# A depthwise convolution split by channels between TensorE and VectorE

## The chip, the cores and the metric

The kernel runs on one core of a Trainium2 chip. The metric is the device time of one execution in microseconds; several runs of a kernel are given by their median. A core has five engines that run side by side, each strictly in the order of its own instruction list, and that wait for each other by semaphores: TensorE (PE; PEld is its loading of weights), VectorE (DVE), ScalarE (ACT), GpSimd (POOL) and SyncE (SP), which here issues transfers.

## The reference

A network of two blocks on 512 tokens of width 1024. The first block (window attention beside a state space model, then a feed-forward with retrieved experts) isn't touched. The second has two layers, each a feed-forward, a mixer with four branches over one projection of the normed input, and a feed-forward. The branches are sparse attention with an index and a top-k ("dsa"), gated linear attention ("gla"), a convolution, and latent attention ("mla"). The branch that is changed, of 256 channels and 31 taps:

```python
def conv_mixer(u, w_dw, b_dw, g_norm):
    a, gate = jnp.split(u, 2, axis=-1)
    h = a * jax.nn.sigmoid(gate)
    h = lax.conv_general_dilated(h, w_dw, window_strides=(1,), padding=[(C_KERNEL - 1, 0)],
                                 feature_group_count=C_CHANNELS, ...) + b_dw
    return jax.nn.silu(rmsnorm(h, g_norm))

def hybrid_layer(x, ...):
    x = x + 0.5 * swiglu(rmsnorm(x, ffn1_norm), ...)
    z = rmsnorm(x, mix_norm) @ w_in                       # split into the branches' inputs
    ...
    y = jnp.concatenate([y_a, y_b, y_c, y_d], axis=-1) @ w_out
    x = x + y
    return x + 0.5 * swiglu(rmsnorm(x, ffn2_norm), ...)
```

Each channel has its own 31 taps: output channel c at token t is a sum over k of tap k of channel c times the same channel's input at token t - 30 + k.

## The kernel before

**Layout.** Activations lie with channels on the 128 partitions and the 512 tokens along the row, so a tile is 128x512 float32 and 256 channels are two tiles ("chunks"). A projection to 128 outputs goes over 8 chunks of the input; each operand is split in a high and a low part of a type that PE takes in one pass, and `mm3` makes three products per chunk, 128x128 by 128x512: high by high (L195), high by low (L196), low by high (L197). A weight block comes by `lw` (L999): a transfer by SP into `wr`, a cast on ACT to `wh` (L1009), a subtraction to `wl` on DVE or POOL (L1010). `wr`, `wh` and `wl` have two buffers each. Products that aren't split are plain float32.

**The mixer** (L1050) runs the steps of a list, `ORDER` (L816): hp, ik, t3, iq, exp, index, lat, mla_in, conv, bqk, v3, gla_in and so on to the four dsa steps, then the output projection "wo". `hp` is `conv_in` (L1519): projection blocks 13 and 15, then 14 and 16, and the gating into `hp`, one tile for both chunks with 30 zero columns ahead of the tokens. `ik`, `t3`, `iq` and `lat` project ("win") and keep a block by a DVE multiplication (`keep`, L1066). `index` makes 24 products (L1234), each followed by a ReLU on ACT (L1236) and a weighting on DVE (L1239, L1241); every fourth is preceded by four copies of queries on ACT (L1232). `topk` (L1251, L1252) is a loop of max and replace on DVE, 16 rounds for each of three blocks. `mla_in` makes the latents' products ("mlain"), `conv` (L1532) is the convolution, both chunks on DVE. `conv_norm` sums squares with a product of ones ("convn"), `silu` works on the gates and the convolution (L1120), and L1303 loads a table of ACT's functions.

**What sets the order.** The steps are written in `ORDER`, but what is printed into each engine's list is chosen by a scheduler with its own estimates of durations, over the whole mixer: an engine's instructions of different steps are interleaved, so `conv` on DVE lies between operations of the index and the projections. A few instructions on ACT, the table loads among them, are held in program order. On the chip nothing is reordered any more. PSUM banks are handed out by tags: "pa" for the projections, "pb", "pc" and "pd" for the branches.

## Time and profile before

| | us |
|---|---|
| Runs, median (lowest to highest of 3) | 3793.75 (3792.79 to 3800.03) |
| The profiled execution | 3798.33 |
| its span, first to last instruction | 3796.5 |
| the first mixer, from its first projection to the last output product | 319.6 |
| the second mixer | 318.2 |
| mean granted clock of TensorE | 0.978 |

The two mixers take 638 of 3796 us. Busy times of an engine are the union of its records; a product's record lasts until its result is out, so records of PE that follow each other closely overlap, and the pace of a row is read from the starts. PEclk is the clock that PE was granted, as a share of 2.4 GHz.

### The profile page before, as it was taken

How to read it: one execution, taken by the hardware profiler on the slowest of the kernel's cores; microseconds unless marked ns; L12 is line 12 of the kernel's file. 1: busy time of each engine (PE TensorE's matmuls, PEld its weight loads, DVE VectorE, ACT ScalarE, POOL GpSimd, SP SyncE). 2: the span in 40 equal slices, each digit the busy share in tenths (PEclk: the TensorE clock that was granted, in tenths of full speed). 3: DMA queues.
4: the chain of work that ended last, by engine and by line, in shares of the span. 5: the costliest groups of instructions: out<-in, count | busy, mean ns of one | idle time of the engine just before them, and what ended most of it. 6: DMA issues, size and time to landing. Idle time of an engine off the chain costs nothing.

```text
span 3796.5 us, 46092 instructions
## 1 busy us (share of the span) xinstructions
PE 3622.3 (95%) x17229; PEld 2972.5 (78%) x17229; DVE 2579.3 (68%) x4508; ACT 1410.8 (37%) x2401; POOL 1087.4 (29%) x677
## 2 busy tenths in 40 slices
PE   7798979899999999999999899999999998999999
PEld 6656879778988888878887576888788875767887
DVE  8668989788888889844445987444444459874443
ACT  3253359423333333342223446222322234463222
POOL 4424767445555555530002212000100013210000
PEclk8899989999999999999999999999999999999999
DMA  4212225888888788723222111223232231112233
GB/s 118 77 39 99 75 98 219 300 290 306 299 295 300 284 309 297 275 93 94 93 96 92 51 45 56 95 95 94 92 95 91 95 94 59 45 51 90 94 95 100
DMA packets 182080, 529.88 MB, mean 140 GB/s; under 512 B 22112, under 2 KB 73888, under 8 KB 163680
## 3 DMA queue, kind: packets, MB, share of 16 engines
q1 hardware_dynamic: 157840, 389.36, 30.9%
q0 software_dynamic: 18944, 134.75, 9.6%
q10 hardware_dynamic: 5072, 2.81, 0.3%
q8 instruction: 136, 2.23, 0.2%
q14 instruction: 88, 0.72, 0.1%
HBM read 495.51 MB, written 30.18 MB: 138 GB/s over the span
## 4 chain that ended last, share of the span: by engine, by line
PE 70%; DVE 10%; issue 2%; DMA 2%; ACT 1%; POOL 1%; ACTq 0%; POOLq 0%; SPq 0%; DVEq 0%
PE ps L197 13%; PE ps L196 13%; PE ps L195 13%; PE V L1820 11%; PE S L195 3%; PE S L197 3%; PE S L196 3%; DVE cv L1541 2%; PE G L1755 2%; PE win L197 1%; PE win L195 1%; PE win L196 1%; DVE ds L1241 1%; DMA gt<-gates 1%; PE wo L195 1%
## 5 line engine op out<-in xcount | busy, mean ns | idle before, releaser
L1009 ACT ACTIVATE wh<-wr 128x1024 fp32r<-128x1024 f32 (+1 forms) x334 | 347.3, 1040 | 1058.3 <-PE ps L196 743.2
L197 PE MATMUL ps<-x,wl 128*128 128x512 f32 x1408 | 557.7, 396 | 0.0
L195 PE MATMUL ps<-x,wh 128*128 128x512 f32 x1408 | 557.4, 396 | 0.0
L196 PE MATMUL ps<-x,wh 128*128 128x512 f32 x1408 | 557.3, 396 | 0.0
L989 POOL TENSOR_TENSOR s<-s,s 128x512 f32<-128x512 f32 x42 | 67.4, 1605 | 1163.9 <-ACT s L987 1152.6
L1811 POOL TENSOR_TENSOR vl<-vr,vh 128x1024 fp32r<-128x1024 f32 x128 | 324.5, 2536 | 182.8 <-ACT vh L1810 181.5
L1010 DVE TENSOR_TENSOR wl<-wr,wh 128x1024 fp32r<-128x1024 f32 (+1 forms) x288 | 343.9, 1194 | 44.4 <-ACT wh L1009 37.7
L197 PE MATMUL S<-pxh,ul 128*128 128x384 f32 x1024 | 350.1, 342 | 9.5 <-POOL ul L1772 9.5
L195 PE MATMUL S<-pxh,uh 128*128 128x384 f32 x1024 | 349.3, 341 | 0.1
L196 PE MATMUL S<-pxl,uh 128*128 128x384 f32 x1024 | 348.9, 341 | 0.0
L195 PEld LDWEIGHTS ps<-x,wh 128*128 128x128 f32 x1408 | 265.5, 189 | 64.6 <-ACT ml L947 1.1
L196 PEld LDWEIGHTS ps<-x,wh 128*128 128x128 f32 x1408 | 265.6, 189 | 63.7 <-issue 0.5
L197 PEld LDWEIGHTS ps<-x,wl 128*128 128x128 f32 x1408 | 265.4, 189 | 63.8 <-issue 0.7
L1820 PE MATMUL V<-vl,ah 128*128 128x512 f32 x768 | 302.8, 394 | 10.3 <-POOL vl L1811 10.2
L1820 PE MATMUL V<-vh,ah 128*128 128x512 f32 x768 | 300.8, 393 | 10.8 <-ACT vh L1810 10.8
L1820 PE MATMUL V<-vh,al 128*128 128x512 f32 x768 | 302.8, 394 | 1.3 <-DVE al L181 1.3
L197 PE MATMUL ps<-ml,wl 128*128 128x512 f32 x704 | 278.0, 395 | 0.0
L195 PE MATMUL ps<-ml,wh 128*128 128x512 f32 x704 | 278.0, 395 | 0.0
L1035 DVE TENSOR_TENSOR s<-ps,rs 128x512 f32<-128x512 f32 x88 | 60.9, 692 | 305.1 <-PE ps L197 305.1
L1881 POOL DMA_INDIRECT rows<-in_uv_dram,gidx x128 | 189.6, 1481 | 259.8 <-DVE acc L1890 229.8
L1047 DVE SCALAR_TENSOR_TENSOR hT<-ps,hT 128x512 f32<-128x512 f32 x96 | 66.4, 692 | 269.1 <-PE ps L197 269.1
L1772 DVE TENSOR_TENSOR ul<-ur,uh 128x1024 fp32r<-128x1024 f32 x100 | 187.9, 1879 | 61.6 <-ACT uh L1770 61.5
(578 smaller groups left out, 7919.3 us busy)
## 6 DMA issues: line engine op xcount, KB each, us to landing
wr<-in_f_gu_dram SPq DMA_DIRECT2D x176, 512.0 KB, 3.7
ur<-in_ut_dram SPq DMA_DIRECT2D x128, 512.0 KB, 5.5
vr<-in_uv_dram SPq DMA_DIRECT2D x128, 512.0 KB, 4.8
wr<-in_f_dn_dram SPq DMA_DIRECT2D x64, 448.0 KB, 3.3
gates<-gst SPq DMA_DIRECT2D x12, 2048.0 KB, 6.9
gt<-gates SPq DMA_DIRECT2D x32, 768.0 KB, 6.9
wr<-in_w_dram SPq DMA_DIRECT2D x46, 512.0 KB, 3.4
wr<-in_f_dn_dram SPq DMA_DIRECT2D x32, 512.0 KB, 3.6
```

What stands on the lines that cost most here:

```text
L195: mm(out, wh, xh, start=start, stop=False)
L196: mm(out, wh, xl, start=False, stop=False)
L197: mm(out, wl, xh, start=False, stop=stop)
L989: nc.gpsimd.tensor_tensor(sq, acc, sq, op=OP.add)
L1009: nc.scalar.activation(hi, raw, AF.Copy)
L1010: (eng or nc.vector).tensor_tensor(lo, raw, hi.bitcast(F32), op=OP.subtract)
L1541: V.scalar_tensor_tensor(a, hp[:, m, k:k + T], dw[:, m, k:k + 1], a, op0=OP.mult, op1=OP.add)
L1755: nc.tensor.matmul(pt[:, t], b[:, t], a, start=True, stop=True)
L1772: e.tensor_tensor(ul, raw, uh.bitcast(F32), op=OP.subtract)
L1811: nc.gpsimd.tensor_tensor(vl, raw, vh.bitcast(F32), op=OP.subtract)
L1820: nc.tensor.matmul(ps[k], x[:, ts], y[:, cs], start=b == 0 and n == 0, stop=b == P - 1 and n == 2)
L1881: nc.gpsimd.indirect_dma_start(r, None, self.A["uv"], bass.IndirectOffsetOnAxis(ap=self.gi[:, s:s + 1], axis=0))
```

## The change

In both mixers the first 128 channels of the convolution (chunk 0) go from DVE to PE, and the other 128 (chunk 1) stay as they were.

- `conv` becomes `conv1` and `conv0`. `conv1` is the old loop for chunk 1. `conv0` makes for each tap k a 128x128 matrix with the tap's 128 weights on the diagonal (ACT scales the identity by a column) and multiplies it with the input shifted by k, in float32; 31 products add up in one PSUM bank ("pd"), and ACT copies the sum out with the bias. The matrices lie in a ring of four within one tile of the tag "sd". `conv0` is called after `conv1`.
- `conv_in` makes chunk 1 first. The two weight blocks that are loaded ahead of the mixer are 14 and 16; 13 and 15 have their low parts on DVE, and 14 and 16 on POOL. `hp` is two tiles, and the taps' transfer is issued at its start.
- `ya`, which reuses the memory of `hp`, is two tiles as well.

All else in the scheduled order follows from this. ACT's list now holds three more table loads between the convolution's norm and the output projection, since the norm's logarithm (L202) and exponential (L203) come to stand between the SiLUs (L1126).

```diff
@@ -1050,12 +1050,12 @@
     def mixer(self, l, x):
         net, nc, w, p = self.net, self.nc, self.w, self.p
         V = nc.vector
-        first = {b: self.lw(self.A["w2"][l, b], 1024) for b in (13, 15)}
+        first = {b: self.lw(self.A["w2"][l, b], 1024) for b in (14, 16)}
         xh, xl, rx = self.scaled(x, "mix")
 
         def proj(b):
             wh, wl = (a.rearrange("p (c m) -> p c m", c=NCH)
-                      for a in first.pop(b, None) or self.lw(self.A["w2"][l, b], 1024, nc.vector if b in (14, 16) else nc.gpsimd))
+                      for a in first.pop(b, None) or self.lw(self.A["w2"][l, b], 1024, nc.vector if b in (13, 15) else nc.gpsimd))
             ps = net.ps("pa", "win")
             for c in range(NCH):
                 net.mm3(ps, (wh[:, c], wl[:, c]), (xh[c], xl[c]), c == 0, c == NCH - 1)
@@ -1103,13 +1103,19 @@
 
         def mla(j):
             if "ya" not in v:
-                v["ya"] = p.tile([P, 2, T + 30], F32, tag="hp", name=net.nm("ya"))[:, :, :T]
+                v["ya"] = [p.tile([P, T + 30], F32, tag=f"hp{m}", name=net.nm("ya"))[:, :T] for m in (1, 0)]
             with net.banks("pb", "mla"):
                 self.mla(j, v["mla"], v["ya"])
 
         def qkn():
             with net.banks("pc", "qkn", rsc):
                 v["rq"] = self.qk_norm(v["qk"])
+        def conv():
+            h0, h1, dw = v["hp"]
+            a = self.conv1(h1, dw)
+            with net.banks("pd", "conv"):
+                v["acc"] = [self.conv0(h0, dw), a]
 
         def conv_norm():
             with net.banks("pd", "convn", rsc):
@@ -1130,7 +1136,7 @@
                     src = v["gla"][m]
                     V.tensor_mul(src, src, v["rg"][m])
                 else:
-                    src = v["ya"][:, m]
+                    src = v["ya"][m]
                 net.split(src, yh[k], yl[k])
 
         def dsa(j):
@@ -1141,7 +1147,7 @@
                 self.dsa(j, v["masks"][j], v["qk"], v["rq"], vt, yh, yl, ("sm", "sd")[j % 2])
 
         steps = {
-            "hp": lambda: v.update(hp=self.conv_in(proj, rx)),
+            "hp": lambda: v.update(hp=self.conv_in(l, proj, rx)),
             "exp": self.exp_set,
             "t3": lambda: v.update(t3=keep(3, "t3")),
             "iq": lambda: v.update(iq=[keep(0, "ds"), keep(1, "ds")]),
@@ -1151,7 +1157,7 @@
             "mla_in": mla_in,
             "bqk": lambda: v.update(bqk=[keep(8, "gl"), keep(9, "gl")]),
             "gla_in": gla_in,
-            "conv": lambda: v.update(acc=self.conv(l, v["hp"])),
+            "conv": conv,
             "qk": lambda: v.update(qk=[keep(b, "ds") for b in (4, 5, 6, 7)]),
             "qkn": qkn,
             "gla": gla,
@@ -1404,7 +1410,7 @@
                 nc.scalar.activation(sm[h][:, :j * P], ps[:, :j * P], AF.Identity, scale=r)
             V.scalar_tensor_tensor(sm[h][:, ts], ps[:, ts], r, self.caus, op0=OP.mult, op1=OP.add)
         self.softmax_pv(sm, n, lambda k, h: kv[k][:, 256 + h * 64:256 + (h + 1) * 64],
-                        lambda c, po: nc.scalar.activation(ya[:, c, ts], po, AF.Copy))
+                        lambda c, po: nc.scalar.activation(ya[c][:, ts], po, AF.Copy))
 
     def gla_in(self, l, bq, bk, t3):
         net, nc, w, p = self.net, self.nc, self.w, self.p
@@ -1516,30 +1522,43 @@
             out.append(o)
         return out
 
-    def conv_in(self, proj, rx):
+    def conv_in(self, l, proj, rx):
         net, nc, w, p = self.net, self.nc, self.w, self.p
-        hp = p.tile([P, 2, T + 30], F32, tag="hp", name=net.nm("hp"))
-        nc.gpsimd.memset(hp[:, :, :30], 0.0)
-        for m in range(2):
+        dw = w.tile([P, 2, 31], F32, tag="dw", name=net.nm("dw"), bufs=1)
+        nc.scalar.dma_start(dw.rearrange("p a b -> p (a b)"), self.A["dw"][l])
+        hp = []
+        for m in (1, 0):
+            h = p.tile([P, T + 30], F32, tag=f"hp{m}", name=net.nm("hp"))
+            nc.gpsimd.memset(h[:, :30], 0.0)
             pa, pg = proj(13 + m), proj(15 + m)
             sg = net.sc(w)
-            nc.vector.tensor_mul(hp[:, m, 30:], pa, rx)
+            nc.vector.tensor_mul(h[:, 30:], pa, rx)
             nc.vector.tensor_mul(sg, pg, rx)
             nc.scalar.activation(sg, sg, AF.Sigmoid)
-            nc.vector.tensor_mul(hp[:, m, 30:], hp[:, m, 30:], sg)
-        return hp
-
-    def conv(self, l, hp):
-        net, nc, w = self.net, self.nc, self.w
-        V = nc.vector
-        dw = w.tile([P, 2, 31], F32, tag="dw", name=net.nm("dw"), bufs=1)
-        nc.scalar.dma_start(dw.rearrange("p a b -> p (a b)"), self.A["dw"][l])
-        acc = self.mts("cv", 2, F32)
-        for m, a in enumerate(acc):
-            V.tensor_scalar(a, hp[:, m, 0:T], dw[:, m, 0:1], self.gv("cb", m), op0=OP.mult, op1=OP.add)
-            for k in range(1, 31):
-                V.scalar_tensor_tensor(a, hp[:, m, k:k + T], dw[:, m, k:k + 1], a, op0=OP.mult, op1=OP.add)
-        return acc
+            nc.vector.tensor_mul(h[:, 30:], h[:, 30:], sg)
+            hp.append(h)
+        return hp[1], hp[0], dw
+    def conv1(self, hp, dw):
+        V = self.nc.vector
+        a = self.mt("cv")
+        V.tensor_scalar(a, hp[:, 0:T], dw[:, 1, 0:1], self.gv("cb", 1), op0=OP.mult, op1=OP.add)
+        for k in range(1, 31):
+            V.scalar_tensor_tensor(a, hp[:, k:k + T], dw[:, 1, k:k + 1], a, op0=OP.mult, op1=OP.add)
+        return a
+    def conv0(self, hp, dw):
+        net, nc = self.net, self.nc
+        ps = net.ps()
+        dg = self.mt("sd").rearrange("p (a k) -> p a k", a=4)
+        for k in range(31):
+            nc.scalar.activation(dg[:, k % 4], net.c("ident"), AF.Identity, scale=dw[:, 0, k:k + 1])
+            nc.tensor.matmul(ps, dg[:, k % 4], hp[:, k:k + T], start=k == 0, stop=k == 30)
+        a = self.mt("cv")
+        nc.scalar.activation(a, ps, AF.Identity, bias=self.gv("cb", 0))
+        return a
 
     def conv_norm(self, acc):
         net, w = self.net, self.w
```

PE's list in the first mixer, from the last transposes of the latents' products ("mlain") to the first product of GLA ("gla"); "win" are projections. Before:

```order
L1386 MATMUL mlain_17807<-cst,sd_17700 96x128
L197 MATMUL win_17953<-x_17003,wl_17949 128x512
L195 MATMUL win_17953<-x_17004,wh_17948 128x512
L196 MATMUL win_17953<-x_17012,wh_17948 128x512
L197 MATMUL win_17953<-x_17004,wl_17949 128x512
L195 MATMUL win_17953<-x_17005,wh_17948 128x512
L196 MATMUL win_17953<-x_17013,wh_17948 128x512
L197 MATMUL win_17953<-x_17005,wl_17949 128x512
L1415 MATMUL gla_17987<-t_3141_17217,gu_17985 128x512
```

The same place after the change:

```order
L1392 MATMUL mlain_17811<-cst,sd_17704 96x128
L197 MATMUL win_17989<-x_17003,wl_17985 128x512
L195 MATMUL win_17989<-x_17004,wh_17984 128x512
L196 MATMUL win_17989<-x_17012,wh_17984 128x512
L1558 MATMUL conv_17850<-hp_17119,sd_17851 128x512 x31
L197 MATMUL win_17989<-x_17004,wl_17985 128x512
L195 MATMUL win_17989<-x_17005,wh_17984 128x512
L196 MATMUL win_17989<-x_17013,wh_17984 128x512
L197 MATMUL win_17989<-x_17005,wl_17985 128x512
L1421 MATMUL gla_18023<-t_3143_17221,gu_18021 128x512
```

All 31 products of the convolution ("conv", from the diagonals in "sd") stand in one row, inside a projection block and ahead of GLA.

DVE's list in the first mixer at the start of the index: "cv" is the convolution, L1066 the keeping of a projection, and L1239 and L1241 (L1245 and L1247 after) the index's weighting. Before:

```order
L1066 TENSOR_TENSOR ds_17283<-win_17290,rs_17055 128x512
L1541 SCALAR_TENSOR_TENSOR cv_17816<-hp_17060,dw_17814,cv_17816 128x512
L1239 TENSOR_SCALAR ds_17324<-r_17331,iw_17317 128x512
L1541 SCALAR_TENSOR_TENSOR cv_17816<-hp_17060,dw_17814,cv_17816 128x512
L1541 SCALAR_TENSOR_TENSOR cv_17817<-hp_17060,dw_17814,cv_17817 128x512
L1241 SCALAR_TENSOR_TENSOR ds_17324<-r_17336,iw_17317,ds_17324 128x512
L1541 SCALAR_TENSOR_TENSOR cv_17816<-hp_17060,dw_17814,cv_17816 128x512
L1241 SCALAR_TENSOR_TENSOR ds_17324<-r_17341,iw_17317,ds_17324 128x512
```

The same place after the change:

```order
L1548 SCALAR_TENSOR_TENSOR cv_17818<-hp_17062,dw_17060,cv_17818 128x512 x3
L1066 TENSOR_TENSOR ds_17287<-win_17294,rs_17055 128x512
L1245 TENSOR_SCALAR ds_17328<-r_17335,iw_17321 128x512
L1247 SCALAR_TENSOR_TENSOR ds_17328<-r_17340,iw_17321,ds_17328 128x512
L1247 SCALAR_TENSOR_TENSOR ds_17328<-r_17345,iw_17321,ds_17328 128x512
L1247 SCALAR_TENSOR_TENSOR ds_17328<-r_17350,iw_17321,ds_17328 128x512
```

The convolution's remaining operations all stand ahead of the index, and none within it any more. Further on in DVE's list, all 48 rounds of top-k now stand ahead of GLA's first operation (L1424; L1418 before), where before most came behind it. On PE, 11 projection products are mixed with the 24 of the index, where 42 were before.

PE's list at the start of the second mixer: "ps" at L197 is the feed-forward's last product, and L992 the sum for the mixer's norm. Before, the sum and the last six of the 12 projection products ahead of it:

```order
L195 MATMUL win_24361<-x_24299,wh_24286 128x512
L196 MATMUL win_24361<-x_24307,wh_24286 128x512
L197 MATMUL win_24361<-x_24299,wl_24287 128x512
L195 MATMUL win_24361<-x_24300,wh_24286 128x512
L196 MATMUL win_24361<-x_24308,wh_24286 128x512
L197 MATMUL win_24361<-x_24300,wl_24287 128x512
L992 MATMUL ps_24352<-s_24349,cst 128x512
```

The same place after the change:

```order
L197 MATMUL ps_24299<-ml_24086,wl_24295 128x512
L992 MATMUL ps_24389<-s_24386,cst 128x512
L195 MATMUL win_24400<-x_24334,wh_24323 128x512
L196 MATMUL win_24400<-x_24342,wh_24323 128x512
L197 MATMUL win_24400<-x_24334,wl_24324 128x512
```

The 12 products that stood ahead of the sum now follow it. In the first mixer 12 stand ahead of it both before and after.

## Rows read from the trace of the kernel before

**Rows 1.** The page, part 1: busy us (share of the span) xinstructions.
```profile
PE 3622.3 (95%) x17229; PEld 2972.5 (78%) x17229; DVE 2579.3 (68%) x4508; ACT 1410.8 (37%) x2401; POOL 1087.4 (29%) x677
```
**Rows 2.** Windows, both mixers: us, busy PE, PEld, DVE, ACT, POOL, PEclk, DMA, GB/s.
```profile
2046.40:2366.00 319.60, 298.51 (x1412) 215.89 (x1411) 269.95 (x546) 159.81 (x329) 74.76 (x34) 0.97 0.17 55
3105.80:3424.00 318.20, 296.85 (x1409) 213.83 (x1408) 272.62 (x542) 159.83 (x328) 74.64 (x33) 0.98 0.17 55
```
**Rows 3.** Windows, the same columns: the five stages of the first mixer.
```profile
2046.40:2097.70 51.30, 46.61 (x196) 36.22 (x194) 40.64 (x44) 15.93 (x17) 14.45 (x6) 1.00 0.26 84
2097.70:2142.00 44.30, 35.98 (x125) 21.74 (x125) 44.30 (x63) 24.39 (x57) 14.02 (x6) 1.00 0.15 48
2142.00:2181.00 39.00, 35.92 (x176) 27.21 (x176) 36.41 (x88) 18.46 (x35) 7.49 (x3) 1.00 0.15 48
2181.00:2286.50 105.50, 101.82 (x532) 74.84 (x530) 92.00 (x235) 53.22 (x116) 21.81 (x9) 0.94 0.13 41
2286.50:2366.00 79.50, 78.19 (x387) 55.89 (x387) 56.60 (x120) 47.80 (x106) 16.98 (x11) 0.98 0.20 60
```
**Rows 4.** Groups, DVE, first mixer: xcount | busy us, mean ns | idle before.
```profile
L1541 DVE SCALAR_TENSOR_TENSOR cv<-hp,dw,cv 128x512 f32<-128x512 f32 x60 | 54.1, 929 | 0.3
L1539 DVE TENSOR_SCALAR cv<-hp,dw,vec 128x512 f32<-128x512 f32 x2 | 3.2, 1587 | 0.0
```
**Rows 5.** Windows, index stage: ACT at L1236, at L1232; PE and PEld at L1234.
```profile
2097.70:2142.00 44.30, 11.49 (x24) 1.00 0.15 48
...
2097.70:2142.00 44.30, 7.34 (x24) 1.00 0.15 48
...
2097.70:2142.00 44.30, 20.45 (x48) 7.65 (x48) 1.00 0.15 48
```
**Rows 6.** PE's timeline: start us, us, records; two windows, ending at 2252 and 2253.6.
```profile
2246.13 0.39 PE L196 MATMUL win<-x,wh 128*128 128x512 f32 x1
2246.36 0.39 PE L197 MATMUL win<-x,wl 128*128 128x512 f32 x1
...
2250.90 1.56 PE L1401 MATMUL mla<-ml,ml 96*128 96x512 f32 x3
...
2250.90 1.98 PE L1401 MATMUL mla<-ml,ml 96*128 96x512 f32 x4
```
**Rows 7.** Groups, ACT, first mixer: columns as in rows 4, with releasers of the idle time.
```profile
L1199 ACT ACTIVATE sm<-sm,st 128x128 f32<-128x128 f32 x4 | 1.5, 388 | 0.0
L1009 ACT ACTIVATE wh<-wr 128x1024 fp32r<-128x1024 f32 x32 | 33.8, 1057 | 43.4 <-PE win L196 28.0 <-issue 7.4 <-PE mlain L229 5.1
L1009 ACT ACTIVATE sm<-wr 128x512 fp32r<-128x512 f32 x2 | 1.3, 630 | 0.0
L1120 ACT ACT_TABLE_LOAD x1 | 1.3, 1283 | 0.0
```
**Rows 8.** Groups, PE, first mixer: columns as in rows 7.
```profile
L195 PE MATMUL win<-x,wh 128*128 128x512 f32 x184 | 79.8, 434 | 3.5 <-DVE t L1066 2.1 <-DVE ds L1066 1.4
```
**Rows 9.** Windows, DVE alone at L1251 (max), then at L1252 (replace): top-k.
```profile
2181.00:2286.50 105.50, 19.13 (x35) 0.94 0.13 41
2046.40:2366.00 319.60, 25.48 (x48) 0.97 0.17 55
...
2181.00:2286.50 105.50, 21.11 (x70) 0.94 0.13 41
2046.40:2366.00 319.60, 28.34 (x96) 0.97 0.17 55
```
**Rows 10.** PE's timeline at the second mixer's start (first and last of 12 products, L992).
```profile
3105.82 0.40 PE L195 MATMUL win<-x,wh 128*128 128x512 f32 x1
...
3108.39 0.40 PE L197 MATMUL win<-x,wl 128*128 128x512 f32 x1
3109.99 1.13 PE L992 MATMUL ps<-s,cst 128*128 128x512 f32 x2 [1.20 <-POOL s L989]
```
**Rows 11.** Windows, columns as in rows 2: the first mixer's last 25 us.
```profile
2341.00:2366.00 25.00, 25.00 (x109) 20.10 (x108) 16.82 (x21) 14.46 (x21) 9.28 (x6) 1.00 0.26 85
```

## Prediction

> **What bounds the kernel now.** I read the page first: TensorE (PE) is busy 95% of the span and VectorE (DVE) 68%, ScalarE (ACT) 37% [rows 1]. That share is a mean over stages, so I cut each mixer out by windows. The change is in the two mixers alone; they take 319.6 and 318.2 us of the span [rows 2]. In the first one I used five stages, cut where the engines' orders cut them [rows 3]: the input projections up to the index (51.3 us), the index products and latents (44.3), the latents' products (39.0), the middle with gated linear attention (GLA), MLA and top-k (105.5), and the rest up to the last product of the output projection (79.5). Three things are to be seen there. In the index stage DVE is busy all 44.3 us and PE only 36.0: DVE sets the pace, as it does nowhere else. In the last two stages, 185 of 319.6 us, PE is busy 97 to 98%, and DVE is not the limit. And the clock that PE was granted stays at 1.00 but for 0.94 and 0.98 in those two. So DVE's relief has a buyer in one stage out of five, while what is put on PE is paid at once unless PE stood still.
>
> **What is taken from DVE.** Per mixer one tensor-scalar (1587 ns) and 30 multiply-adds (929 ns on average) go, half of the two chunks [rows 4]: (54.1 + 3.2) / 2 = 28.6 us of DVE.
>
> **What is put on PE.** 31 products of a 128x128 matrix with 128x512 float32, in one unbroken row. A float32 product leaves two records: the 24 index products are read by 24 activations and have 48 records [rows 5]. In a row, each further 512-column float32 record adds 0.42 us (three took 1.56 us, four 1.98) [rows 6], against 0.23 between starts for the projections' products. So 31 x 2 x 0.43 = 26.7 us (62 x 0.42 = 26.0 at the low end; 0.455 a record, with gaps for the ring of four diagonals, gives 28.2), and 0.6 for entering and leaving the row: **+27.3**. The two records are there because the operands are float32; the projections have one record each. ACT's 31 diagonals are 128x128, as the 388 ns scaled copy of that shape [rows 7]: 31 x 0.39 = 12 us, under 27 us of PE, so PE is the slower side of the ring. ACT stands still in between, and behind the diagonals wait the casts of the next weight blocks; before, ACT's casts waited 28.0 us for PE in this mixer as it was, for the ring of two weight buffers to come free [rows 7]. The block that PE is in the middle of has its weights. I cost this at nothing; if that cover is gone, a cast of 1.0 us and a DVE or GpSimd subtraction stand in PE's way once.
>
> **What comes back, stage by stage.** *Projections before the index:* PE waits 3.5 us in all for DVE's products that free its banks [rows 8]. DVE has fewer multiply-adds ahead of them (30 instead of 36 ahead of the last), and the first pair of blocks is subtracted elsewhere: -2.5 (-1.5 to -4). *Index and latents:* DVE's conv no longer stands between its index operations. What is left as the pace is the chain of one product, one activation and the next: 11.5 us of ReLUs and 7.3 of query copies on ACT [rows 5] and three casts of 0.63 [rows 7] make 20.7; PE's side of it is 16.5 to 19 (20.45 us [rows 5] less a tail of 0.16, i.e. 0.39 - 0.23 [rows 6], on each of 24 products). In the new order only 11 projection products are mixed into the index, and 61 follow it: 61 x 0.232 = 14.2, and 1.5 for entry. 21 + 14.2 + 1.5 = 36.7 against 44.3: -7.6 (-4 to -11). *Latents' products:* 0 (-2 to 2); DVE is at 93% there, but PE's waits are for ACT and GpSimd too. *Middle:* DVE loses all the top-k of this stage, 19.1 + 21.1 = 40.2 us [rows 9], since it now does the 48 rounds ahead of GLA. But PE was idle only 3.7 us there, and at a granted clock of 0.94 it had 12.7 us at 1.2 GHz, which cost half, 6.3. A denser row of products may win part of these 10: -5 (0 to -12). *Last stage:* idle 1.3 and 1.6 us lost to the clock; against that, three more table loads of 1.28 us [rows 7] stand on ACT in the chain from conv's norm to the output projection: +1 (-2 to +4). Sum: 27.3 - 2.5 - 7.6 - 5 + 1 = **+13.2** per mixer. Counting the middle's gain at nothing gives 18, all of it 8.
>
> *Second mixer only:* PE had 12 projection products, 2.8 us, ahead of the norm's sum (L992), and still waited 1.2 us for GpSimd [rows 10]. In the new order the sum stands first, so the 2.8 us become waiting: **+2.8**, less if GpSimd's chain starts earlier. In the first mixer the order there is unchanged.
>
> *On GpSimd and the queues:* one more memset of 30 columns, and the taps' transfer moves to the mixer's start; nobody waits for either in the trace. I cost these at 0.
>
> Total 2 x 13.2 + 2.8 = 29 us. The profiled execution took 3798.3 us (a span of 3796.5), 4.6 above the median of 3793.75; its stages scale by one part in a thousand, so I add the 29 to the median: **3823**.
>
> **Bounds.** To come out even, 27.3 us have to be found per mixer. The idle time with no product in flight is 319.6 - 298.5 = 21.1 us and 318.2 - 296.9 = 21.3 [rows 2]; with 8 us lost to the clock, 29. Tails of waiting products are counted as busy, so it is no strict limit, but a change that is even has to win nearly all of it.
>
> **The rivals.** *(a) DVE's relief is the gain (faster).* If DVE's chain sets the end, and PE's busy time is mostly latency, then the products fall into room that is there and 28.6 us go from each mixer: 3794 - 57 = 3737; with half of it, 3765 to 3780. For it: DVE's 84% of the mixer [rows 2] and the index stage. Against it: stages 4 and 5, where DVE has 13.5 and 23 us free and PE next to none. Weight loads are busy 216 of 319.6 us, 68% [rows 2]. The Trainium skill, "Perfetto Trace Analysis", § Identifying the Most-Contended Engine, has it that matmul busy time is a bad measure because products are pipelined, and that the share of weight loads is a good one; by that PE would have a third of the mixer free, DVE would be the more contended engine, and (a) would hold at about 3737. The trace speaks against using it so here: in the last 25 us of the mixer PE runs without one gap, and weight loads stand at 20.1 of 25 us, 80% [rows 11]; so 80% is full here, and 68% of it leaves 15% of the mixer, 48 us, not all of which can be reached. I give (a) 0.10.
> *(b) Waits give it all back (no change).* Index -11, projections -4, middle -12: 27 per mixer; with the 2.8 about 3797. It needs every stage at its best end: 0.13.
> *(c) Worse than the sum (slower still).* ACT is held for the row's 27 us, GLA's operands come late from DVE (top-k now stands ahead of GLA: by the sums of its instructions DVE gets there about 5 us before PE, and a few GpSimd collisions use that up), or PE's clock falls in the sparser index: no gain in the middle and 5 us more per mixer give 2 x 23 + 2.8 + 10 = about 3853: 0.12.
> *(d) The products don't take 0.42 a record.* Back to back like the projections' 0.23 they would be 14.4 us: 2 x (14.4 + 0.6 - 14.1) + 2.8 = 3798, which falls into (b)'s time. The float32 rows of this trace exclude it, and I count it there.
>
> **How the numbers follow.** The sum: 0.65; (a) 0.10, (b) with (d) 0.13, (c) 0.12. The sum's own range is 3805 to 3838. About 0.2%, 7.6 us, is what a measurement of this kernel can tell from no change. (b) lies between 3786 and 3801 for the most part; (c) up to 3860. For 8 in 10 I leave out (a) and the outer ends of (b) and (c): 3793 to 3850. Faster 0.10; same 0.14, with (b) and the sum's rim; slower 0.76.
>
> **What would show it.** In the changed kernel's profile: 62 records in a row at about 0.43 us, no wait within; PE's share of the index stage up from 81% and that stage shorter by 4 to 11 us; DVE's share of a mixer down to about 72%; no top-k after GLA's first operation; GLA's start about 17 us later than the 2180.7 us at which the middle begins here; and a wait near 4 us ahead of the second mixer's L992. It is wrong if the row is shorter than 26 us, if the index stage does not shrink, or if the middle gains or loses over 12 us.

## The result, and the profile after

The changed kernel takes 3861.0 us (median of four runs, 3856.5 to 3865.5); before, in the same comparison, 3796.1. The ratio is 1.017, 95% interval 1.0155 to 1.0185: 65 us more, where 29 were forecast, and above the range's upper end of 3850. The sign was right, the size was not. A second comparison on another chip gave 1.0156 (1.0131 to 1.0181).

The profiled execution took 3859.8 us with a span of 3858.1, 61.6 more than the one before, and the two mixers hold all of it. The windows of the changed kernel, first the stages of its first mixer (the entry to GLA in its middle), then the two mixers, the second cut at the end of the feed-forward ahead of it, then the second mixer's entry to GLA and all behind it (columns: us, busy PE, PEld, DVE, ACT, POOL, granted clock, DMA share, GB/s):

```profile
2045.90:2098.70 52.80, 48.03 (x195) 37.09 (x193) 41.83 (x44) 16.57 (x20) 14.67 (x6) 0.97 0.25 82
2098.70:2137.00 38.30, 36.52 (x125) 21.43 (x125) 33.67 (x77) 23.84 (x55) 10.97 (x6) 1.00 0.17 55
2137.00:2172.40 35.40, 33.96 (x169) 25.90 (x169) 32.88 (x75) 17.43 (x33) 7.26 (x3) 1.00 0.16 53
...
2172.40:2218.20 45.80, 40.34 (x112) 21.38 (x110) 39.91 (x94) 19.61 (x45) 4.94 (x2) 0.93 0.04 13
...
2218.20:2314.00 95.80, 91.76 (x522) 67.99 (x522) 49.94 (x123) 52.34 (x115) 17.05 (x7) 0.98 0.13 44
2314.00:2388.20 74.20, 72.02 (x345) 51.24 (x346) 51.28 (x103) 44.83 (x97) 16.23 (x11) 0.98 0.18 58
...
2045.90:2388.20 342.30, 322.62 (x1462) 225.03 (x1461) 249.53 (x512) 174.63 (x361) 71.12 (x35) 0.98 0.16 51
3130.40:3483.70 353.30, 329.32 (x1462) 229.23 (x1462) 249.25 (x509) 174.81 (x361) 70.98 (x33) 0.95 0.15 49
...
3262.10:3307.50 45.40, 39.94 (x112) 21.06 (x110) 39.91 (x94) 19.59 (x44) 4.94 (x2) 0.92 0.04 12
3307.50:3483.70 176.20, 169.96 (x865) 123.19 (x866) 100.95 (x222) 97.42 (x211) 33.12 (x16) 0.94 0.15 48
```

These answer to [rows 2] and [rows 3]. For an exact difference both kernels are cut at the same events of PE: the first index transpose, the first product and the last transpose of the latents, the first product of GLA's running sums (L1445 before, L1451 after), the last output product. "Entry to GLA" is the stretch that holds the row of 31 products after the change. Before, the entry and all behind it read, in the first mixer and then in the second:

```profile
2179.10:2193.60 14.50, 12.42 (x55) 8.73 (x53) 14.07 (x37) 6.96 (x13) 4.80 (x2) 1.00 0.19 58
2193.60:2363.60 170.00, 167.09 (x861) 121.38 (x862) 133.89 (x324) 93.24 (x208) 33.62 (x17) 0.95 0.16 49
...
3238.20:3252.70 14.50, 12.42 (x55) 8.77 (x53) 14.04 (x37) 7.00 (x13) 4.78 (x2) 1.00 0.19 59
3252.70:3422.10 169.40, 164.92 (x861) 119.22 (x862) 137.14 (x321) 93.61 (x208) 33.21 (x16) 0.97 0.15 48
```

| stage, us | first mixer: before, after | | second mixer: before, after | | forecast |
|---|---|---|---|---|---|
| projections | 51.1, 52.8 | +1.7 | 51.1, 56.4 | +5.3 | -2.5; second mixer +0.3 |
| index and latents | 44.4, 38.3 | -6.1 | 44.4, 39.9 | -4.5 | -7.6 |
| latents' products | 37.0, 35.4 | -1.6 | 36.9, 35.4 | -1.5 | 0 |
| entry to GLA, with the row | 14.5, 45.8 | +31.3 | 14.5, 45.4 | +30.9 | row +27.3 |
| the rest | 170.0, 170.0 | 0 | 169.4, 176.2 | +6.8 | -4 with the entry's waits |
| sum | 317.0, 342.3 | +25.3 | 316.3, 353.3 | +37.0 | +13.2; +16.0 |

The row is what it was forecast to be: its 62 records cover 26.8 us, their mean is 592 ns, and PE waits for nothing within it. The group's row, and ACT's 31 diagonals:

```profile
L1558 PE MATMUL conv<-hp,sd 128*128 128x512 f32 x62 | 26.8, 592 | 0.0
...
L1557 ACT ACTIVATE sd<-cst,dw 128x128 f32<-128x128 f32 x31 | 12.1, 400 | 11.8 <-PE conv L1558 11.8
```

So 53.6 of the 62.3 us are the row. The misses are elsewhere: with the latents' products 7.7 and 6.0 us came back behind the projections, where 7.6 were forecast, but the projections gave nothing, 4.5 and 4.1 us more than the row were lost at the entry to GLA, and the rest gave nothing.

What happens at that entry is in the chain of waits from the end of the latents' products to PE's next wait, by line (the view itself breaks off at the end):

```profile
by line: DVE ds L1258 42.2%; DVE m L1257 37.8%; DVE sd L1300 8.6%; DVE sd L1298 4.2%; DVE ds L1259 1.9%; DVE rg L1066 1.8%; ACT ml L1394 1.7%; issue 1.6%; PE vtr L1085 1.4%; DVE tr L217 0.5%; ACT tr L215 0.3%; DVE rqd L1388 0.2%; DVE tr L22
```

80% of it is top-k on DVE (L1257, L1258); the row of products isn't in it at all. PE was through with its row (2199.8) before DVE was through with the 48 rounds (2200.5). First, for comparison, GLA's first operations on PE and DVE before, then the timelines of PE and of DVE at that point after the change:

```profile
2180.68 1.12 PE L1415 MATMUL gla<-t,gu 16*128 16x512 f32 x2
...
2181.84 0.75 DVE L1418 TENSOR_SCALAR gl<-gla,vec 128x512 f32<-128x512 f32 x1 [0.25 <-PE gla L1415]
...
2200.62 1.12 PE L1421 MATMUL gla<-t,gu 16*128 16x512 f32 x2
2201.67 0.51 PE L195 MATMUL win<-x,wh 128*128 128x512 f32 x1
2205.99 0.90 PE L1085 MATMUL vtr<-cst,rg 128*128 128x128 f32 x3 [3.81 <-DVE rg L1066]
...
2199.79 0.68 DVE L1258 MATCH_REPLACE8 ds<-m,ds 128x512 f32<-128x512 f32 x1
2200.50 0.43 DVE L1259 TENSOR_SCALAR ds<-ds 128x512 f32<-128x512 f32 x1
2201.03 0.42 DVE L1298 TENSOR_TENSOR sd<-bias,ds 128x256 f32<-128x256 f32 x1
2201.37 0.35 DVE L1300 TENSOR_SCALAR sd<-ds,b 128x256 f32<-128x256 f32 x1
2201.64 0.42 DVE L1298 TENSOR_TENSOR sd<-bias,ds 128x256 f32<-128x256 f32 x1
2201.97 2.43 DVE L1300 TENSOR_SCALAR sd<-ds,b 128x256 f32<-128x256 f32 x1
...
2205.26 0.68 DVE L1066 TENSOR_TENSOR rg<-win,rs 128x512 f32<-128x512 f32 x1
2205.86 0.34 DVE L1300 TENSOR_SCALAR sd<-ds,b 128x256 f32<-128x256 f32 x1
2206.12 0.74 DVE L1424 TENSOR_SCALAR gl<-gla,vec 128x512 f32<-128x512 f32 x1
```

PE waits 3.81 us for DVE to keep a block of values (L1066). Behind the last round of top-k stand, ahead of that keep, the bias additions of the sparse attention (L1298, L1300). One of them takes 2.43 us where the one before took 0.35. GpSimd is at a subtraction in those 2 us; it had waited 33.42 us for ACT's cast, which stood behind the row's diagonals. DVE's first operation of GLA needs PE's first product of it, and begins 5.50 us behind that product's start, where it was 1.16 before: DVE is 4.3 us late. From GLA's first product to the end of the stretch PE takes 17.6 us at a clock of 0.81, where it took 12.9 at 1.00. The subtraction:

```profile
2201.68 2.58 POOL L1010 TENSOR_TENSOR wl<-wr,wh 128x1024 fp32r<-128x1024 f32 x1 [33.42 <-ACT wh L1009]
```

The Trainium skill, "SBUF — State Buffer", § SBUF: two separate sides, says that VectorE, in operations of certain forms, and GpSimd share one pair of ports as an exclusive lock, so that the later of the two stands still until the other's instruction is done; the trace agrees (2.43 against 0.35 us, ending within 0.15 us of GpSimd's end).

In the second mixer, the sum at L992 waits 4.00 us where it waited 1.20 before [rows 10]:

```profile
3130.22 0.40 PE L197 MATMUL ps<-ml,wl 128*128 128x512 f32 x1
3134.62 2.08 PE L992 MATMUL ps<-s,cst 128*128 128x512 f32 x2 [4.00 <-POOL s L989]
...
3132.70:3139.50 6.80, 4.88 (x10) 3.23 (x11) 0.74 (x2) 2.58 (x3) 1.76 (x1) 0.51 0.22 77
```

The last line is a window: from within that wait on, PE was granted 0.51 of its clock, 1.2 GHz, for 6.8 us.

### The profile page after: what moved, and what is told of

Same layout as the page of the kernel before. It is cut to its first block, busy times and chain, and to the rows that moved or that the text cites. A ratio compares the mean times of both kernels' runs of the same rounds, so it can differ in the third digit from the quotient of the medians.

```text
span 3858.1 us, 46387 instructions
## 1 busy us (share of the span) xinstructions
PE 3676.9 (95%) x17353; PEld 2994.8 (78%) x17353; DVE 2537.0 (66%) x4446; ACT 1444.1 (37%) x2471; POOL 1079.6 (28%) x679
## 4 chain that ended last, share of the span: by engine, by line
PE 69%; DVE 10%; ACT 2%; DMA 2%; issue 2%; POOL 1%; ACTq 0%; POOLq 0%; SPq 0%; DVEq 0%
PE ps L195 13%; PE ps L197 13%; PE ps L196 13%; PE V L1839 11%; PE S L195 3%; PE S L196 3%; PE S L197 3%; PE G L1774 2%; DVE cv L1548 2%; DVE ds L1258 1%; DVE m L1257 1%; PE win L196 1%; PE win L197 1%; PE win L195 1%; DMA vr<-in_uv_dram 1%
## 5 line engine op out<-in xcount | busy, mean ns | idle before, releaser
L197 PE MATMUL ps<-x,wl 128*128 128x512 f32 x1408 | 557.1, 396 | 0.0
L1010 DVE TENSOR_TENSOR wl<-wr,wh 128x1024 fp32r<-128x1024 f32 (+1 forms) x288 | 343.7, 1193 | 44.3 <-ACT wh L1009 37.6
L197 PE MATMUL S<-pxh,ul 128*128 128x384 f32 x1024 | 349.6, 341 | 8.0 <-POOL ul L1791 8.0
L197 PEld LDWEIGHTS ps<-x,wl 128*128 128x128 f32 x1408 | 265.1, 188 | 63.8 <-issue 0.7
L197 PE MATMUL ps<-ml,wl 128*128 128x512 f32 x704 | 277.9, 395 | 0.0
L1010 POOL TENSOR_TENSOR wl<-wr,wh 128x1024 fp32r<-128x1024 f32 x46 | 112.9, 2455 | 458.4 <-ACT wh L1009 343.9
```

The source lines that it names most:

```text
L197: mm(out, wl, xh, start=False, stop=stop)
L1010: (eng or nc.vector).tensor_tensor(lo, raw, hi.bitcast(F32), op=OP.subtract)
```

## The experiments

The kernel before and each experiment ran in turn on one chip, so each is given by its ratio to before there, with a 95% interval. "..." in the code marks lines that are left out.

**The changed kernel again.** No edit.

> The changed kernel once more, beside the three below on one chip: 1.017 of before, and the same waits and clock stretches in its middle if they belong to the kernel and not to one execution.

3860.1, ratio 1.0156 (1.0131 to 1.0181). The entry to GLA took 46.2 us at a clock of 0.93, as in the first profile. The loss belongs to the kernel.

**Chunk 0 back on DVE, the other edits kept.**

```diff
-            nc.scalar.activation(dg[:, k % 4], net.c("ident"), AF.Identity, scale=dw[:, 0, k:k + 1])
-            nc.tensor.matmul(ps, dg[:, k % 4], hp[:, k:k + T], start=k == 0, stop=k == 30)
...
+            V.scalar_tensor_tensor(a, hp[:, k:k + T], dw[:, 0, k:k + 1], a, op0=OP.mult, op1=OP.add)
```

> The changed kernel with chunk 0 back on DVE; all its other edits stay (chunk 1 first, other weight blocks ahead, two tiles for hp and ya, the taps' transfer early). PE's list is that of before, row for row. Theory A (the loss comes from the products on PE and from the order that they bring): 3796, within 5 us of before. Theory B (the accompanying edits cost, for instance the clock loss of 1.4 us and the later L992): above 3805.

Ratio 1.0002 (0.9992 to 1.0011). In sum the accompanying edits cost nothing. They do move time between stages: the projections of this kernel's first mixer take 52.6 us at a clock of 0.97, as in the changed kernel, so the 1.7 us lost there are not the row's.

**The kernel before without chunk 0, and the changed kernel without its products.** Two ways to take 30 multiply-adds of DVE per mixer away, 28 us by the mean of [rows 4], and put nothing or next to nothing on PE.

```diff
# no_chunk0, on the kernel before
-            for k in range(1, 31):
+            for k in range(1, 31 if m else 1):
# no_products, on the changed kernel
-        for k in range(31):
+        for k in range(1):
...
```

> The kernel before with chunk 0's 30 multiply-adds left out, the first tap kept (so chunk 0's branch is not the reference's). It prices DVE's relief alone, 27.9 us per mixer, with no product added. Theory A (PE sets the end but for the index stage): the index and latents' stages give 6 to 8 us per mixer, so 3780 to 3784. Theory B (DVE is the bound of the mixer): 2 x 28 us less, about 3740.

> The changed kernel with 30 of the 31 taps of chunk 0 left out on PE (one diagonal, one product; chunk 0's branch is not the reference's). Everything else of the change stays. Theory A (the loss is the row of products and the order that it makes; the rest of the change is worth what the kernel without chunk 0 is worth): 3789 to 3796. Theory B (the accompanying edits or ACT's part hold some of the loss when no DVE work of chunk 0 hides it): above 3800.

0.9988 (0.9978 to 0.9997), and 0.9954 (0.9938 to 0.9971). Chunk 0 taken off DVE in both mixers is worth 5 to 17 us in all, even when the work vanishes; rival (a) of the prediction is out. Theory B of both is out, but neither theory A hit its size: the first gained less, the second more. And in the first, the place that theory A named gave nothing. Its index and latents take 45.2 us, no less than before, with 12 multiply-adds of chunk 1 still between the index's operations and 19 projection products in it, not 11:

```profile
2089.70:2134.90 45.20, 37.31 (x125) 22.30 (x125) 41.34 (x77) 24.59 (x57) 12.00 (x6) 0.96 0.16 47
```

With the changed kernel's order and no products the stage takes 38.4 us, and with all of the convolution on DVE but behind the index (below) 37.5. So the shorter index comes from the order that the scheduler makes, not from less work on DVE as such.

**One pass instead of float32.**

```diff
-        dg = self.mt("sd").rearrange("p (a k) -> p a k", a=4)
+        dg = self.mt("sd", F32R).rearrange("p (a k) -> p a k", a=4)
...
-            h = p.tile([P, T + 30], F32, tag=f"hp{m}", name=net.nm("hp"))
+            h = p.tile([P, T + 30], F32 if m else F32R, tag=f"hp{m}", name=net.nm("hp"))
...
```

> The changed kernel with chunk 0's input and the diagonals rounded to the type that PE takes in one pass (so the convolution is less exact): each of the 31 products costs 0.232 us instead of 0.86, 7.2 per mixer instead of 26.7. Theory A (the products are paid on PE one to one): 19.5 us less per mixer, 3822, and down to 3815 if DVE is no longer late for GLA. Theory B (the loss is the order and ACT's 31 diagonals, 12 us, rather than PE's time): 3845 to 3861.

3817.6, ratio 1.0055 (1.0039 to 1.0072): about 1% or 40 us below the changed kernel, against 39 that the products are shorter by the expectation's prices. PE's time is paid about one to one. The products are no longer one row here, and 29 rounds of top-k instead of 48 stand ahead of GLA, so it isn't the row's length alone: the entry is 22 us shorter in either mixer, and DVE is on time for GLA there. What is left, 0.55% or 21 us, is the products' remaining 14 us and 7 more; none of DVE's relief shows.

**The row twice.**

```diff
-            nc.tensor.matmul(ps, dg[:, k % 4], hp[:, k:k + T], start=k == 0, stop=k == 30)
+            nc.tensor.matmul(ps, dg[:, k % 4], hp[:, k:k + T], start=k == 0, stop=False)
+            nc.tensor.matmul(ps, dg[:, k % 4], hp[:, k:k + T], start=False, stop=k == 30)
...
+        nc.scalar.activation(a, ps, AF.Identity, bias=self.gv("cb", 0), scale=0.5)
```

> The changed kernel with each of the 31 products made twice (the sum is halved by the copy out), 62 in the row; the order on every engine is otherwise the same. A second 26.6 us per mixer. Theory A (the row is paid in full, but DVE's 48 rounds of top-k reach beyond its end and GLA waits 4 to 7 us for them): the second row covers that wait, so 2 x (26.6 - 4 to 7): 39 to 45 us more than the changed kernel. Theory B (paid in full and nothing is hidden): 53 more. Theory C (PE has room in the row's surroundings): under 30 more.

3897.4, ratio 1.0252 (1.0232 to 1.0273): 37 us more than the changed kernel beside it, where the products add 53. The windows of the entry, the changed kernel first (beside it on the chip), then with the row twice:

```profile
2175.50:2221.70 46.20, 40.72 (x112) 21.66 (x110) 39.97 (x94) 19.55 (x44) 4.95 (x2) 0.93 0.04 13
```

```profile
2171.20:2237.30 66.10, 64.58 (x173) 31.28 (x172) 37.91 (x94) 19.58 (x44) 4.76 (x2) 1.00 0.03 9
```

19.9 us more for 26.8 us of products: 6.9 us of the second row lie where PE stood still or ran at half clock. Its waits for the values fell from 5.5 to 2.1 us. Theory A, slightly below its range; B and C are out. DVE, through with top-k, now stands still at the fourth bias addition until the row ends, since that addition writes a tile of the tag "sd", as the row's diagonals do:

```profile
2225.59 0.43 DVE L1298 TENSOR_TENSOR sd<-bias,ds 128x256 f32<-128x256 f32 x1 [23.91 <-PE conv L1559]
```

It is on time for GLA again (1.16 us behind PE's first product), and no addition meets a subtraction of GpSimd.

**Fewer rounds of top-k.**

```diff
-        for _ in range(16):
+        for _ in range(12):
```

> The changed kernel with 12 rounds of top-k per block instead of 16 (the masks keep fewer keys, so the sparse attention is another one): 36 rounds, still all ahead of GLA, PE's list almost unchanged. DVE is 12 rounds of 1.12 us, 13 us, earlier at GLA. Theory A (DVE is late for GLA by 4 to 8 us per mixer): that wait goes, and 9 to 16 us come back in all, 3845 to 3851. Theory B (the wait at GLA's start is for something else): 3860.

3851.5, ratio 1.0126 (1.0105 to 1.0148), so 0.3 to 0.4% or 11 to 17 us below the changed kernel's two comparisons; its interval ends 0.07% below the first's and overlaps the second's. At the entry the trace shows it without that doubt: PE's list is nearly the same, and the entry has

```profile
2177.30:2217.30 40.00, 38.49 (x113) 19.71 (x111) 26.62 (x61) 19.52 (x45) 4.77 (x2) 1.00 0.04 15
```

40.0 us for 45.8, at full clock, near the 14.5 + 26.8 = 41.3 of "before plus the row". The wait at the values in the whole mixer, in the changed kernel and then here (before: 1.6 us):

```profile
L1085 PE MATMUL vtr<-cst,rg 128*128 128x128 f32 x16 | 3.0, 316 | 5.5 <-DVE rg L1066 5.5
```

```profile
L1085 PE MATMUL vtr<-cst,rg 128*128 128x128 f32 x16 | 2.6, 283 | 2.0 <-DVE rg L1066 2.0
```

DVE now has 8.45 us to spare when the row ends, and its first GLA operation again begins 1.15 us behind PE's first product:

```profile
2204.70 0.42 DVE L1298 TENSOR_TENSOR sd<-bias,ds 128x256 f32<-128x256 f32 x1 [8.45 <-PE conv L1558]
...
2205.99 1.12 PE L1421 MATMUL gla<-t,gu 16*128 16x512 f32 x2
...
2207.14 0.75 DVE L1424 TENSOR_SCALAR gl<-gla,vec 128x512 f32<-128x512 f32 x1 [0.36 <-PE gla L1421]
```

So the excess at the entry is DVE's top-k, which leaves the additions behind it, and the collision of one of them with GpSimd, to the time after the row.

**Top-k moved behind GLA**, all of it, then one block of three pinned.

```diff
-            V.max(m8, acc)
...
+            a = V.max(m8, acc)
+            if not i:                      # part_of_topk: only for block j = 1
+                self.tc.keep_in_program_order(a)
```

> The changed kernel with every block's top-k held behind the DVE work written ahead of it, so all 48 rounds come after GLA's operations on DVE. Theory A (DVE comes late to GLA since top-k stands ahead of it): the waits of the values' transposes (5.5 us) and of GLA's products go, 5 to 8 us per mixer, 3845 to 3851, unless top-k then comes late for the sparse attention. Theory B (the middle is long for another reason): 3861 or more, with the same waits.

> The changed kernel with the top-k of one block alone (the one with j = 1) held behind the DVE work written ahead of it: by DVE's list 16 rounds stand ahead of GLA and 32 behind, where 48 stand ahead in the changed kernel. Theory A (DVE is late for GLA): GLA starts as early as with all top-k behind it, and the sparse attention is not starved: 3846 to 3852. Theory B (top-k must be done in the row's shadow or it delays the sparse attention): above 3870.

1.0418 (1.0401 to 1.0436) and 1.0277 (1.0259 to 1.0295): the first is far above its theory A and waits elsewhere than its theory B said, the second is its theory B. The entry does shrink, to 38.8 us with all of it behind, 7 less than in the changed kernel; but the sparse attention then waits for its masks. The longest wait of PE near the end of the first mixer, in either kernel (us in total, times, longest):

```profile
PE wo L196 <- DVE x L181: 20.9, 1, 20.9
```

```profile
PE dsa L1305 <- DVE sm L1306: 16.7, 1, 16.7
...
2329.50:2363.60 34.10, 17.32 (x50) 8.81 (x51) 31.17 (x89) 9.40 (x28) 0.25 (x2) 0.50 0.05 16
```

The second fence's last line is a window of the kernel with one block pinned: 34 us at half clock, PE busy for 17. So the rounds have to be done before the sparse attention, and the row's shadow is not a bad place; it is only too short.

**The row behind GLA.**

```diff
-ORDER = "... v3 gla_in v2 v0 gla mla0 ...".split()       # the row was in the step "conv"
+ORDER = "... v3 gla_in v2 v0 gla row mla0 ...".split()
...
```

> The changed kernel with the row of 31 products as a step of its own, written behind GLA instead of ahead of it. On DVE 27 rounds of top-k instead of 48 then stand ahead of GLA; the row still is 31 products in one piece. Theory A (the row's place makes DVE late for GLA): the 21.4 us from the end of the latents' products' successor, GLA's first product, to L1451 fall to some 14, and 7 us per mixer come back: 3846. Theory B (each product of the row is paid and nothing else matters): 3861.

1.0145 (1.0128 to 1.0162): 0.1 to 0.25% below the changed kernel, within the intervals. In the first mixer the entry, without the row, takes 16.9 us, 2.4 above before, with a wait of 3.9 us for the values in it (5.1 in the mixer). In the second it takes 14.6 us, as before, and the values wait 0.6. The row takes its 27 us where it is. Undecided in time: the gain that theory A named came at one entry and not in the whole.

**The diagonals on GpSimd.**

```diff
-            nc.scalar.activation(dg[:, k % 4], net.c("ident"), AF.Identity, scale=dw[:, 0, k:k + 1])
+            nc.gpsimd.tensor_scalar(dg[:, k % 4], net.c("ident"), dw[:, 0, k:k + 1], None, op0=OP.mult)
```

> The changed kernel with the 31 diagonals made on GpSimd instead of ACT; PE's and DVE's lists stay. Theory A (the ring holds ACT for the row's length and that costs nothing): within 5 us of the changed kernel, as long as GpSimd makes a diagonal in under 0.86 us. Theory B (ACT, held for 27 us, delays weight casts and GLA): 5 to 10 us per mixer less, 3841 to 3851.

1.0155 (1.0135 to 1.0176), the changed kernel's own: theory A. ACT's being held costs nothing that its freedom would give back. Even the collision stays (one addition of 2.43 us): ACT's cast ahead of GpSimd's subtraction then waits for PE.

**The convolution elsewhere.** All of it on DVE but behind the index; chunk 0 on ACT and GpSimd; on GpSimd; half of it on GpSimd.

```diff
# conv_behind_index, on the kernel before
+            self.tc.keep_in_program_order(V.tensor_scalar(a, hp[:, m, 0:T], dw[:, m, 0:1], ...))
# chunk0_on_act_pool (the first tap, with the bias, left out here)
+            nc.scalar.activation(s, hp[:, k:k + T], AF.Identity, scale=dw[:, 0, k:k + 1])
+            nc.gpsimd.tensor_tensor(a, a, s, op=OP.add)
# chunk0_on_pool (half_on_pool: k < 16, the rest on DVE)
+                nc.gpsimd.tensor_scalar(s, hp[:, k:k + T], dw[:, 0, k:k + 1], None, op0=OP.mult)
+                nc.gpsimd.tensor_tensor(a, a, s, op=OP.add)
```

> The kernel before, all of the convolution on DVE, but each chunk's first operation held behind the DVE work written ahead of it: the 62 operations come behind the index and the latents' products, and 27 rounds of top-k come ahead. Theory A (the index stage is worth 6 us per mixer once the convolution is out of it, and the middle has room on DVE): 3785 to 3790. Theory B (whatever is taken out of the index stage comes back as a late GLA): 3795 to 3820.

> A version that puts nothing on PE: chunk 0's taps as scaled copies on ACT (31 of some 0.7 us) and additions on GpSimd (30 of 1.6 us, 48 us per mixer). Theory A (PE sets the end; DVE's relief is worth what the kernels without chunk 0 gained, 0.1 to 0.5%, if ACT and GpSimd have room): 0.995 to 0.999 of before. Theory B (the slower chain on ACT and GpSimd delays weights or the convolution's norm): 1.01 or more.

> A version that puts chunk 0 on GpSimd alone: 31 scalings and 30 additions per mixer (at 1.3 us for an addition some 70 to 80 us), nothing on PE, ACT or DVE. Theory A (the 0.1 to 0.5% that the kernels without chunk 0 gained can be had if the work goes to an engine with room and no wait for it): 0.995 to 0.999 of before. Theory B (GpSimd makes low parts of weights, and those come late behind the taps): 1.005 or more.

> As the one before, with taps 0 to 15 of chunk 0 on GpSimd and the other 15 on DVE behind them: half the work on GpSimd. Theory A: 0.997 to 1.000 of before. Theory B (late weights): above 1.003, but less than with all of it on GpSimd.

1.0174 (1.0155 to 1.0193), 1.0157 (1.0136 to 1.0177), 1.0204 (1.0184 to 1.0225), 1.0179 (1.0158 to 1.0199): none beats the kernel before. The last three are their theory B; that half on GpSimd costs less than all of it is not shown, since the intervals overlap. The first is slower than both its theories. Each has long waits of PE in its first mixer that the kernel before hasn't; one kind of each, in this order (us in total, times, longest):

```profile
PE gla L1496 <- DVE qb L1491: 20.1, 4, 9.3
```

```profile
PE win L195 <- ACT wh L1009: 26.2, 1, 26.2
```

```profile
PE win L197 <- POOL wl L1010: 25.4, 3, 13.6
```

```profile
PE vtr L1085 <- DVE rg L1066: 18.2, 2, 17.5
```

A block of cheap operations in an engine's fixed list holds up what stands behind it: GLA's operands on DVE, the casts of weights on ACT, the low parts of weights on GpSimd.

## Why the prediction was wrong, point by point

- **The row** (forecast +27.3): right, 26.8 us, with no wait of PE in it and ACT under it.
- **DVE's relief** (28.6 us): too high. The chunks' multiply-adds were priced at their mean of 929 ns, which holds collisions with GpSimd (last section); between the windows of [rows 2] and those above DVE's busy time fell by 20.4 and 23.4 us per mixer. The sum doesn't use this term, rival (a)'s price does.
- **Index and latents** (-7.6): the size -6.1 and -4.5, within the bounds given, and the latents' products gave 1.5 more. The mechanism that the prediction named, no convolution between the index's operations and fewer projection products in it, fits the runs; they don't separate the two, and leaving chunk 0 out alone gave nothing here.
- **The middle** (-5, with the last stage -4): the step that failed. It booked the 40 us of top-k that leave the stage as DVE's gain and asked only what PE could take of it. It didn't cost where those rounds went: ahead of GLA, the last of them under the row, in which DVE has 27 us, is busy for all of them and isn't through at the end. The working held that DVE would reach GLA some 5 us ahead of PE and left the other case to rival (c); the trace has DVE's first GLA operation (L1424) 5.5 us behind PE's (2206.1 against 2200.6), 4.3 more than before, and 2.1 of these are the collision with GpSimd, which only rival (c) reckoned with. That is +4.5 and +4.1 at the entry, shown by the row made twice and by the twelve rounds. With what lies behind the entry, this step makes 23.4 of the 33.1 us by which the two mixers exceed the forecast; the projections make 9.2.
- **The rest behind the entry**: 0 in the first mixer, +6.8 in the second. In the second, its windows read 0.94 of the clock over 176.2 us and 0.97 over 169.4 before. By the lost share of either window that is 10.6 against 5.1 us, so some 5 of the 6.8 are the clock: an estimate, as no run sets the clock alone. In the first, by the same estimate, the clock gave back some 5 us (0.98 for 0.95); against that PE stood idle for 6.2 us instead of 2.9, 2.2 of them in a wait of GLA's products for DVE (L1502 for L1497) that wasn't there before.
- **Projections** (-2.5, in the second mixer +2.8 for L992): L992 right to the sign and size of its wait (4.00 for 1.20 us), but the recovery of 2.5 didn't come: the mixer's first stage shows a clock of 0.97 and 0.94 where it was 1.00, 1.6 and 3.4 us by the same estimate. The 0.97 comes with the accompanying edits, without any row.
- **No cost for the taps' transfer, ACT and the other edits**: right in sum, by the kernels with chunk 0 back on DVE and with the diagonals on GpSimd. The table loads were not tested on their own.
- **Rivals.** (a), DVE as the bound, is excluded: chunk 0 gone from DVE is worth 0.1 to 0.5%, not 1.5%. The Trainium skill's rule on judging TensorE by its weight loads ("Perfetto Trace Analysis", § Identifying the Most-Contended Engine) would have led to it; here PEld was at 68% of the mixer before, and no kernel of this case found that third. (c) is what happened, a little beyond its 3853 to 3860, and for one of the three reasons that it gave: GLA's operands late from DVE. ACT's being held cost nothing, and the clock did fall, but not in the index, where (c) put it (1.00 there). It had 0.12; given a working that put DVE 5 us from being late, it deserved far more.

What stays open: the changed kernel is 1.6 to 1.7% slower, and its version without the products 0.5% faster. The 2.1% between are 80 us (61 to 94 by the intervals); the two profiled executions are 70 apart. Cut at the same events, 30.0 and 29.6 of these lie at the two entries, where the 60 products left out make 51.6 and DVE's lateness most of the rest, and 1.6 and 11.7 lie behind them. In the second mixer, behind the entry, the version without the products ran at full clock, where the changed kernel has 0.94 over 176.2 us:

```profile
3249.20:3413.70 164.50, 159.40 (x858) 115.95 (x859) 120.50 (x276) 93.79 (x208) 33.01 (x16) 1.00 0.16 49
```

The order differs between the two as well, and no run separates the clock from the waits that precede it.

## What to carry to other kernels

Before moving work off an engine, leave the work out and time that: here 28 us per mixer, as priced, were worth 2 to 9, and what is put on the bound engine in exchange must cost less than that. When an instruction list is fixed ahead, ask what the relieved engine will do in the time it gains, and who stands behind that: top-k filled the room and made the next stage late. Work in one block on an engine that feeds others must be priced at what queues behind it, not at its own busy time.

## What the runs showed of the hardware

Long waits came with half the clock, so that the work behind them was slower too. In the kernel with the convolution behind the index, PE waited for DVE in the middle of the first mixer (13.6 us for a block of values, 20.1 in four waits for GLA's operands), and the windows read (us, busy PE and others, clock):

```profile
2200.80:2217.90 17.10, 6.83 (x22) 4.38 (x23) 17.10 (x31) 2.49 (x4) 1.02 (x1) 0.50 0.10 31
2217.90:2224.70 6.80, 4.39 (x27) 2.77 (x25) 6.79 (x13) 1.06 (x1) 1.80 (x1) 0.99 0.00 0
2224.70:2272.50 47.80, 29.37 (x115) 21.68 (x116) 33.73 (x75) 7.04 (x20) 0.78 (x1) 0.50 0.04 12
```

65 us at 1.2 GHz with PE busy for 36 of them. The longest such stretch in the kernel before's mixers was 6.8 us. The collision of DVE and GpSimd seen above also raises the mean of the convolution's multiply-adds, 1080 ns in the changed kernel's first mixer and 929 before [rows 4]. Those that meet no operation of GpSimd take 751 and 740 ns on average; 5 of 30 after and 6 of 60 before, each beside a subtraction of GpSimd (L1010), take 2.2 to 3.0 us. So taking half of these operations away does not save half of their time.
